# The context block moved to second place in the first layer, and a later start for the next modulation

## The chip, the cores and the metric

The program runs on one core of one Trainium2 chip. The core has five engines that work side by side, each through its own queue in order: PE (TensorE, the matrix unit), DVE (VectorE), ACT (ScalarE), POOL (GpSimd) and SP, which here only starts transfers. Transfers (DMA) are started from the queues of SP and ACT. The metric is the time of one execution on the device in microseconds (us); smaller is better. Three runs of the kernel before were timed, and one execution was profiled.

## The reference

Two layers work on 2048 latent tokens and 256 context tokens of 1024 values. Each layer makes shift, scale and gate out of a condition vector (the modulation: `silu(c) @ w_mod + b_mod`), normalises the tokens, projects them with one matrix, runs four mixers, gates their outputs and projects them back:

```
h = rmsnorm(x) * (1 + scale) + shift            # latent by c, context by c_ctx
parts = split(h @ w_in)                          # q, k, v, z_a, u_f, z_f, b, c, h, z_c, u_p, z_p
o_att = silu(z_a) * attention(q, k, v)           # latent reads context + latent, context reads context
o_f   = silu(z_f) * (real(fft2(u_f)) @ w_fourier)
o_c   = silu(z_c) * (b * conv3(c * h))
o_p   = silu(z_p) * pooled(u_p)
x = x + gate * (concat(o_f, o_att, o_c, o_p) @ w_out)
```

The second layer needs of the context only its keys and values, and only the latent tokens are returned. So the context's output (attention, local mixers, projection) is computed in the first layer alone.

## The kernel before

The tokens lie in five blocks: block 0 is the context (256 tokens), blocks 1 to 4 are 512 latent tokens each. Products of f32 accuracy are made of three f16 matmuls (`PASSES`). A layer runs in these stages, and generators hand each stage's work out in small steps, so that two stages can be woven together:

- **Token groups**: `prep` normalises and transposes a block, `token_groups` makes queries, keys, values and the Fourier input and writes them to DRAM (`qd`, `kd`, `vd`, `ud`).
- **Gates with Fourier** (`gate_groups`, `fourier`): the gates are 148 steps of six 128x512 matmuls on PE (L319). The Fourier mixer is 24 steps: for each of two halves nine output rows (`emit`, L753), then six mixing steps. Each `emit` step splits its operands on ACT and DVE (`split_r`, L687 and L688) and runs a few small matmuls (`dft`, L711). `spread` (L1216) puts 136 of the gate steps between the 24 Fourier steps, and `issue_after` ties the order of the two kinds of matmuls on PE: the gate matmuls of one step stay behind the Fourier matmuls of a step some four places earlier.
- **Modulation of later use** (`modulate`, L163): in the first layer, eight columns of modulation run in the same stage, handed out by `weave` (L1227). Each of 32 steps loads 512 KB of `w_mod` (SP queue, L175) and multiplies it by the condition on two streams: the first on DVE (L182, L184); the second on ACT (L187, into one buffer `part`), added up on POOL (L189). Only PE's instructions are tied by `issue_after`; those of DVE, ACT, POOL and SP are put where the scheduler of the framework finds them ready, the earlier traced first.
- **Attention with local mixers and the first part of the projection** (`attention`, `local_groups`, `project`): for each block and each of four heads, `Head.front` finds the largest score of each query row (matmul L958, reduction on DVE L959; 20 such products for a latent block, 2 for the context), and `Head.main` goes over the keys (18 tiles of 128, the context 2), with two exponentials on ACT and the difference of the two on POOL or DVE. The front of the next head is spread over the main loop of the present one, six units ahead. `spread` puts fill steps between: gates left over, local mixers, then the projection of the blocks in `early`.
- **Rest of the projection with the next layer's token groups**: the last two of `blocks` (`late`) are projected while the next layer's tokens are prepared.

The order of the blocks in attention and projection is the list `blocks`, in which the context stood last:

```
blocks = sorted(layer_blocks(L), key=lambda b: b == 0)     # 1, 2, 3, 4, 0
early = blocks[:-2]                                        # 1, 2, 3
late = project(L, blocks[-2:], ...)                        # 4, 0
```

The number of fill steps in attention is `m - 20`, with m growing by a sixteenth of the tokens of `early`. `set_gate` (L1118) makes the gate row of one stream by two f32 matmuls (L1125) and two ACT copies (L1126), and `project` calls it when the stream of the tokens changes. `local_groups` goes by `layer_blocks(L)`, that is 0 to 4.

Of the kernel before, what the change touches and what calls it, by code (L numbers as in the profile page):

```python
# [42 lines left out]
def hybrid_kernel(ctx: ExitStack, tc: tile.TileContext, T, out):  # L43
# [24 lines left out]
    def ring(*tags):  # L68
        i = [0]

        def bank(dt=F32):
            i[0] += 1
            tag = tags[i[0] % len(tags)]
            return banks[tag].tile([128, 2048 // mybir.dt.size(dt)], dt, tag=tag, name=tag)

        return bank

    st_bank, mx_bank, pv_bank, fl_bank = (ring(t) for t in ("st", "mx", "pv", "fl"))
# [149 lines left out]
    def alloc_h(b):  # L228
        n = BLK[b][1]
        per = 2048 // n  # L230
        hT[b] = [[big([128, per, n], F16, f"h{b}{part}{i}") for i in range(KC // per)] for part in range(2)]

    def h_ap(b, part, k, t0, n, nk=1):
        per = 2048 // BLK[b][1]
        t = hT[b][part][k // per]
        return t[:, k % per, t0:t0 + n] if nk == 1 else t[:, k % per:k % per + nk, t0:t0 + n]

    def rms_scale(ss, n, count, tag):
        ms = sm.tile([128, 8], F32, tag=tag, name=tag)[:, 0:n]
        POOL.tensor_scalar(out=ms, in0=ss, scalar1=1.0 / count, scalar2=EPS, op0=ALU.mult, op1=ALU.add)  # L240
        POOL.tensor_tensor(out=ms, in0=ms, in1=nh[:, 0:n], op=ALU.pow)
        return ms

    def prep(L, b, tp, psum):

        s = 1 if b == 0 else 0
        g0, n = BLK[b]

        def load(t):
            xt = tp.tile([128, D], F32, tag="x", name="xt")  # L250
            (SP if L == 0 and b < 2 else ACT).dma_start(out=xt, in_=source(L, g0 + t * 128))
            return xt

        ahead = load(0)
        for t in range(n // 128):
            xt = ahead
            if (t + 1) * 128 < n:
                ahead = load(t + 1)
            xn = tp.tile([128, D], F32, tag="xn", name="xn")
            ss = sm.tile([128, 1], F32, tag="ss", name="ss")  # L260
            ACT.activation(out=xn, in_=xt, func=ACTF.Square, accum_out=ss)
            rstd = rms_scale(ss, 1, D, "rx")
            ACT.activation(out=xn, in_=xt, func=ACTF.Copy, scale=rstd)
            yield
            if t == 0:
                alloc_h(b)
            for half in range(2):
                pt = psum()
                for j in range(4):
                    k = 4 * half + j  # L270
                    PE.transpose(out=pt[:, j * 128:(j + 1) * 128], in_=xn[:, k * 128:(k + 1) * 128], identity=id32)
                h32 = tp.tile([128, 4, 128], F32, tag="h32", name="h32")
                for j in range(4):
                    k = 4 * half + j
                    DVE.tensor_scalar(out=h32[:, j, :], in0=pt[:, j * 128:(j + 1) * 128], scalar1=aff[L][0][:, 0, k, s:s + 1],
                                      scalar2=aff[L][0][:, 1, k, s:s + 1], op0=ALU.mult, op1=ALU.add)
                hi = h_ap(b, 0, 4 * half, t * 128, 128, 4)
                ACT.copy(out=hi, in_=h32)
                POOL.tensor_tensor(out=h_ap(b, 1, 4 * half, t * 128, 128, 4), in0=h32, in1=hi, op=ALU.subtract)  # L279
# [74 lines left out]
    def layer_blocks(L):  # L354
        return list(range(5)) if L == 0 else list(range(1, 5))
# [773 lines left out]
    def source(L, tok):  # L1129

        if L > 0:
            return xd[tok:tok + 128]
        return T["ctx"][tok:tok + 128] if tok < NCTX else T["x"][tok - NCTX:tok - NCTX + 128]
# [42 lines left out]
    def steps(gen, n):  # L1176
        for _ in range(n):
            if next(gen, 0) == 0:
                return

    def chain(*gens):
        for g in gens:
            yield from g
# [4 lines left out]
    with ExitStack() as st:  # L1188
        tp = TagPool(st, tc, "s0", {**TOKEN, "x": 4, "xn": 2, "h32": 2, "row": 1})
        ws = []  # L1190
        ahead = prep(0, 0, tp, aux_bank)
# [16 lines left out]
        for b in range(5):  # L1208
            ahead = prep(0, b + 1, tp, aux_bank) if b + 1 < 5 else iter(())
# [14 lines left out]
            with tc.issue_after(past[0]), tc.issue_after(load_mark[0] or past[0]):  # L1224
                steps(fill, n * (i + 1) // total - n * i // total)

    def weave(gen, n, other, m):  # L1227

        for i in range(n):
            steps(gen, 1)  # L1230
            steps(other, m * (i + 1) // n - m * i // n)
            yield
        yield from gen
        yield from other

    def opening(load, att):

        for _ in load:
            steps(att, 3)
            yield 1  # L1240

    for L in range(DEPTH):
        blocks = sorted(layer_blocks(L), key=lambda b: b == 0)
        nb = len(blocks)
        GATES = 148 * nb // 5
        zst = ExitStack()
        w_mode(f"g{L}", False)
        gates = gate_groups(L, TagPool(zst, tc, f"z{L}", {"z": 1}), gate_w[L])
        with ExitStack() as st:
            tags = {"acc0": 1, "acc1": 1, "part": 1} if L == 0 else {}  # L1250
            tags.update({"u": 5, "wf": 1, "wm": 2, "t32": 3, "td": 3, "osb": 1, "dtab": 1, "tab": 1, "pq800": 1, "pq801": 1, "pq810": 1, "pq811": 1})
            if L:
                tags.update({"dtab": 2, "tab": 2, "td": 4})
            fp = TagPool(st, tc, f"f{L}", tags)
            mods = chain(*(modulate(i, c, pv_bank, fp) for i, c in ([(0, 4), (0, 5)] + [(1, c) for c in range(6)] if L == 0 else [])))
            work = weave(fourier(L, fp), 24, mods, 32)
            steps(gates, 12)
            spread(work, gates, 24, GATES - 12, 4, True)
            steps(work, 1 << 30)
            if L == 0:  # L1260
                affine(1)
        right = ExitStack()
        ap = TagPool(right, tc, f"a{L}", {"zt": 2, "p32": 2, "qb": 2, "qhh": 3, "qlm": 2, "ph": 3, "pl": 3, "acc": 1, "o32": 1}, "right")
        kvs = {}
        att = attention([Head(L, kvs, b, h, ap) for b in blocks for h in range(4)])
        with ExitStack() as st:
            lp = TagPool(st, tc, f"l{L}", {"e": 8, "ht": 2, "hb": 2, "hu": 2, "pw32": 1, "pw": 2, "dh": 1, "dl": 1})
            early = blocks[:-2]
            out1 = project(L, early, big, 1)
            fill = chain(gates, local_groups(L, lp, out_weights(L), lambda: project_setup(L, kvs, 1), out1), out1)  # L1270
            load = keys_values(L, ap, kvs)
            steps(fill, 5)
            spread(load, fill, 5, 10, 0, True)
            spread(opening(load, att), fill, 6, 18, 1, True)
            n = 28 - 18 + sum(72 if b else 8 for b in blocks)
            m = 2 * 8 * 4 * nb - GATES + 3 - 15 - 18 + sum(BLK[b][1] // 16 for b in early)
            spread(att, fill, n, m - 20, 1)
            project_setup(L, kvs, 2)
            steps(att, 1 << 30)
        zst.close()  # L1280
        right.close()
        with ExitStack() as st:
            pp = TagPool(st, tc, f"p{L}", {"mix": 1, "ml": 2, "gate": 1, "x": 2})
            late = project(L, blocks[-2:], lambda shape, dt, name: pp.tile(shape, dt, "mix" if name == "dg" else name, name), 2)
            steps(late, 1)
            steps(fill, 1 << 30)
            if L + 1 < DEPTH:
                w_mode(f"t{L + 1}", True)
                with ExitStack() as st2:
                    sp = TagPool(st2, tc, f"s{L + 1}", {**TOKEN, "s": 2, "x": 2, "xn": 1, "h32": 2}, "right")  # L1290
                    with tc.issue_after(load_mark[0]):
                        block = token_groups(L + 1, sp, [])
                    for b in blocks[0:2]:
                        for _ in prep(L + 1, b, sp, mx_bank):
                            steps(late, 3)
                    for i, b in enumerate(blocks):
                        ahead = prep(L + 1, blocks[i + 2], sp, mx_bank) if i + 2 < 5 else iter(())
                        if i == 3:
                            gate_w[L + 1] = load_w(L + 1, *GATE_W[0:2], True)
                        for _ in block(b):  # L1300
                            steps(ahead, 1)
                            steps(late, 8)
                        steps(ahead, 9)
                        if i == 0:
                            steps(late, 1 << 30)
            steps(late, 1 << 30)
# [98 lines left out]
```

## Time and profile before

| what | value |
|---|---|
| median of 3 runs | 2219.25 us (2217.25 to 2222.85) |
| the profiled execution's own time | 2221.17 us |
| its span, first to last instruction | 2219.4 us |
| PE busy | 2136.6 us, 96% of the span |
| DVE, ACT, POOL busy | 1411.0, 1216.8, 931.7 us |
| mean granted TensorE clock | 0.990 |

Read it so: PE is busy nearly all the time, and what is not busy is 82.8 us in small pieces. The granted clock is 1.0 (2.4 GHz) but for a few stretches at 0.5 (1.2 GHz), which stand inside the busy time.

### The profile page before, as it was taken

How to read it: one execution, taken by the hardware profiler on the slowest of the kernel's cores; microseconds unless marked ns; L12 is line 12 of the kernel's file. 1: busy time of each engine (PE TensorE's matmuls, PEld its weight loads, DVE VectorE, ACT ScalarE, POOL GpSimd, SP SyncE). 2: the span in 40 equal slices, each digit the busy share in tenths (PEclk: the TensorE clock that was granted, in tenths of full speed). 3: DMA queues.
4: the chain of work that ended last, by engine and by line, in shares of the span. 5: the costliest groups of instructions: out<-in, count | busy, mean ns of one | idle time of the engine just before them, and what ended most of it. 6: DMA issues, size and time to landing. Idle time of an engine off the chain costs nothing. (4 is left out here: it accounts for less than half of the span.)

```text
span 2219.4 us, 41113 instructions
## 1 busy us (share of the span) xinstructions
PE 2136.6 (96%) x16207; PEld 1287.1 (58%) x16207; DVE 1411.0 (64%) x2661; ACT 1216.8 (55%) x2265; POOL 931.7 (42%) x998
## 2 busy tenths in 40 slices
PE   7999989989999999999899999999999999989999
PEld 3998545655556555555456995555455555555544
DVE  3654777456687878676575554522678787877533
ACT  4653445346677767555554534334477676766600
POOL 2786543214455556233233862001356355543300
PEclk9999989999999999999999999999999999999999
DMA  8433554551212122222454333335221221223133
GB/s 324 141 101 96 178 165 160 203 155 48 65 46 69 58 71 79 95 71 69 171 200 134 118 100 114 110 105 169 71 65 33 68 63 46 72 88 99 42 102 123
DMA packets 182639, 237.95 MB, mean 107 GB/s; under 512 B 47178, under 2 KB 132526, under 8 KB 182446
## 3 DMA queue, kind: packets, MB, share of 16 engines
q1 hardware_dynamic: 159854, 205.96, 28.4%
q10 hardware_dynamic: 22592, 29.37, 4.2%
q8 instruction: 127, 2.08, 0.4%
q14 instruction: 66, 0.54, 0.1%
HBM read 161.48 MB, written 69.34 MB: 104 GB/s over the span
## 5 line engine op out<-in xcount | busy, mean ns | idle before, releaser
L319 PE MATMUL fl<-h,w 128*128 128x512 f16 (+1 forms) x2592 | 595.5, 368 | 0.4 <-ACT z L504 0.2
L1007 POOL TENSOR_TENSOR pl<-p,ph 128x512 f16<-128x512 f32 (+1 forms) x292 | 355.2, 1216 | 517.9 <-ACT p L1006 435.0
L319 PEld LDWEIGHTS <-w 128*128 128x128 f16 x3456 | 331.2, 99 | 362.0 <-issue 38.8
L1005 ACT ACTIVATE ph<-st 128x512 f16<-128x512 f32 (+1 forms) x584 | 348.7, 597 | 239.2 <-PE st L1001 213.3
L959 DVE TENSOR_REDUCE mp<-mx 128x1 f32<-128x512 f32 (+1 forms) x648 | 394.7, 627 | 114.4 <-PE mx L958 111.7
L1166 PE MATMUL fl<-wo,ml 128*128 128x512 f16 x1632 | 378.9, 380 | 1.4 <-ACT gate L1126 1.1
L1006 ACT ACTIVATE p<-st 128x512 f32<-128x512 f32 (+1 forms) x584 | 349.0, 598 | 25.2 <-DVE pl L1007 23.7
L1007 DVE TENSOR_TENSOR pl<-p,ph 128x512 f16<-128x512 f32 (+1 forms) x292 | 233.1, 798 | 83.5 <-ACT p L1006 67.9
L1166 PEld LDWEIGHTS <-ml 128*128 128x128 f16 x1632 | 158.9, 98 | 184.2 <-issue 6.4
L995 PEld LDWEIGHTS <-ph 128*128 128x128 f16 x2320 | 169.6, 98 | 124.3 <-ACT ph L1005 26.8
L995 PE MATMUL pv<-V,ph 128*128 128x130 f16 x2320 | 222.7, 220 | 11.3 <-ACT ph L1005 10.9
L958 PE MATMUL mx<-kst,qhh 128*128 128x512 f16 x512 | 188.1, 379 | 15.2 <-DVE mp L959 12.2
L319 PE MATMUL st<-h,w 128*128 128x512 f16 (+1 forms) x864 | 195.4, 376 | 3.6 <-DVE r L436 3.6
L1000 PE MATMUL st<-qhh,kst 128*128 128x512 f16 x512 | 193.9, 379 | 2.5 <-ACT p L1006 2.3
L1001 PE MATMUL st<-qlm,k 65*128 65x512 f16 x512 | 195.1, 381 | 0.0
L993 PE MATMUL pv<-V,pl 128*128 128x66 f16 x2320 | 169.1, 193 | 4.1 <-DVE pl L1007 2.1
L342 PEld LDWEIGHTS <-h 128*128 128x128 f16 x1632 | 159.9, 98 | 20.6 <-POOL h L279 0.7
L993 PEld LDWEIGHTS <-pl 128*128 128x128 f16 x2320 | 132.6, 97 | 44.0 <-POOL pl L1007 6.0
L1171 DVE TENSOR_TENSOR fl<-fl,gate 128x512 f32<-128x512 f32 x68 | 47.4, 697 | 99.8 <-PE fl L1166 99.7
L145 POOL TENSOR_TENSOR root<-root,ph__105 128x2 f32<-128x2 f32 (+1 forms) x28 | 20.3, 726 | 207.6 <-DVE root L144 197.7
L157 ACT ACTIVATE ml<-mix,f 128x1024 f16<-128x1024 f32 x34 | 39.1, 1151 | 113.6 <-PE fl L1166 80.3
L332 PEld LDWEIGHTS <-h 128*128 128x128 f16 x1728 | 98.5, 98 | 0.7
(300 smaller groups left out, 3024.4 us busy)
## 6 DMA issues: line engine op xcount, KB each, us to landing
wm<-in_w_mod_dram SPq DMA_DIRECT2D x48, 512.0 KB, 4.5
wst<-in_w_in_dram SPq DMA_DIRECT2D x44, 512.0 KB, 4.2
mix<-mixd SPq DMA_DIRECT2D x34, 512.0 KB, 4.4
zd<-z SPq DMA_DIRECT2D x64, 256.0 KB, 2.2
wst<-in_w_out_dram SPq DMA_DIRECT2D x32, 512.0 KB, 4.5
xd<-x SPq DMA_DIRECT2D x18, 512.0 KB, 3.0
xt<-xd ACTq DMA_DIRECT2D x18, 512.0 KB, 4.4
x<-in_x_dram SPq DMA_DIRECT2D x16, 512.0 KB, 5.2
```

The costliest lines, as they stand in the source:

```text
L319: last = PE.matmul(out=ps, lhsT=w[:, wp, k, :], rhs=h_ap(b, hp, k, 0, n), start=(k == 0 and i == 0), stop=(k == KC - 1 and i == 2))
L342: PE.matmul(out=ps[:, t], lhsT=h_ap(b, hp, k, (2 * i + t) * 128, 128), rhs=w[:, :, wp, k, :], start=(k == 0 and j == 0), stop=(k == KC - 1 ...
L958: mark[0] = PE.matmul(out=ps, lhsT=qhh[:, t * 128:(t + 1) * 128], rhs=kk, start=True, stop=True).ins
L959: DVE.tensor_reduce(out=mp[:, t, i:i + 1], in_=ps, axis=AX.X, op=ALU.max)
L993: PE.matmul(out=pv[t // 2][:, t % 2, 0:66], lhsT=p, rhs=v[:, 0:66], start=False, stop=(kt == nk - 1), skip_group_check=True)
L995: PE.matmul(out=pv[t // 2][:, t % 2, :], lhsT=p, rhs=v, start=(kt == 0 and t % 2 == 0), stop=False, skip_group_check=True)
L1000: mark[0] = PE.matmul(out=ps, lhsT=self.k_tile(0, kt), rhs=qhh, start=True, stop=False).ins
L1001: PE.matmul(out=ps, lhsT=self.k_tile(1, kt)[0:65, :], rhs=qlm[0:65, :], start=False, stop=True)
L1005: ACT.activation(out=ph, in_=ps, func=ACTF.Exp, scale=1.0 / LOGIT)
L1006: ACT.activation(out=p32, in_=ps, func=ACTF.Exp, scale=1.0 / LOGIT)
L1007: (POOL if kt % 2 == 0 else DVE).tensor_tensor(out=pl, in0=p32, in1=ph, op=ALU.subtract)
L1166: PE.matmul(out=ps, lhsT=ml[:, mp, k, :], rhs=wo[k][:, wp, half * 512:(half + 1) * 512], start=(k == 0 and j == 0), stop=(k == KC - 1 and ...
```

## The change

In the first layer the list of blocks becomes 1, 0, 2, 3, 4, so the context comes second in attention, `early` becomes 1, 0, 2 and `late` 3, 4. The next layer's token groups keep their order 1, 2, 3, 4, 0 through a list of its own. `local_groups` itself is not touched by the diff. `weave` gets a parameter: the modulation's 32 steps are handed out over the Fourier steps 6 to 23 in place of 0 to 23.

```diff
-    def weave(gen, n, other, m):
+    def weave(gen, n, other, m, alone):
 
         for i in range(n):
             steps(gen, 1)
-            steps(other, m * (i + 1) // n - m * i // n)
+            if i >= alone:
+                steps(other, m * (i + 1 - alone) // (n - alone) - m * (i - alone) // (n - alone))
             yield
...
     for L in range(DEPTH):
-        blocks = sorted(layer_blocks(L), key=lambda b: b == 0)
+        blocks = [1, 0, 2, 3, 4] if L == 0 else layer_blocks(L)
+        order = [1, 2, 3, 4, 0]
...
-            work = weave(fourier(L, fp), 24, mods, 32)
+            work = weave(fourier(L, fp), 24, mods, 32, 6)
...
-                    for b in blocks[0:2]:
+                    for b in order[0:2]:
                         for _ in prep(L + 1, b, sp, mx_bank):
                             steps(late, 3)
-                    for i, b in enumerate(blocks):
-                        ahead = prep(L + 1, blocks[i + 2], sp, mx_bank) if i + 2 < 5 else iter(())
+                    for i, b in enumerate(order):
+                        ahead = prep(L + 1, order[i + 2], sp, mx_bank) if i + 2 < 5 else iter(())
```

## Rows read from the trace of the kernel before

**Rows 1.** The page, part 1: busy time, share of the span, instructions.

```profile
PE 2136.6 (96%) x16207; PEld 1287.1 (58%) x16207; DVE 1411.0 (64%) x2661; ACT 1216.8 (55%) x2265; POOL 931.7 (42%) x998
```

**Rows 2.** Stretches: us, busy us (instructions) per engine, clock, DMA share, GB/s.

```profile
240.40:244.05 3.65, 0.00 (x0) 0.00 (x1) 1.20 (x7) 1.32 (x4) 2.82 (x2) 1.00 0.61 180
244.50:251.30 6.80, 6.36 (x24) 4.47 (x24) 4.14 (x14) 3.00 (x6) 0.76 (x2) 0.50 0.48 158
284.70:299.10 14.40, 10.19 (x52) 5.07 (x51) 14.40 (x33) 7.54 (x14) 7.57 (x6) 1.00 0.52 174
299.10:312.80 13.70, 12.48 (x49) 8.99 (x50) 9.35 (x22) 4.86 (x11) 3.67 (x3) 0.50 0.55 177
500.00:1035.00 535.00, 524.59 (x4248) 299.25 (x4247) 404.76 (x653) 351.77 (x676) 253.44 (x258) 1.00 0.21 66
1074.00:1095.00 21.00, 17.15 (x120) 9.54 (x118) 12.82 (x43) 8.14 (x25) 6.60 (x12) 0.99 0.21 71
1094.40:1097.80 3.40, 2.92 (x7) 1.02 (x7) 0.73 (x3) 1.27 (x3) 0.78 (x2) 0.50 0.70 224
1097.80:1200.00 102.20, 101.51 (x559) 56.00 (x558) 64.91 (x136) 53.41 (x75) 34.78 (x44) 1.00 0.55 184
1200.00:1335.00 135.00, 135.00 (x1624) 123.59 (x1623) 68.03 (x164) 54.50 (x92) 91.07 (x106) 1.00 0.34 107
```

**Rows 3.** Timeline around the first Fourier matmul: start, us, engine, line, idle before.

```profile
239.90 2.79 POOL L189 TENSOR_TENSOR acc<-acc,part 128x512 f32<-128x512 f32 x1 [1.98 <-ACT part L187]
240.29 0.48 DVE L728 TENSOR_TENSOR tr<-ftmp 128x128 f32<-128x128 f32 x2
242.73 0.72 ACT L187 ACTIVATE part<-wm,sc 128x512 f32<-128x512 f32 x1 [2.90 <-POOL acc L189]
244.05 0.51 PE L711 MATMUL mx<-tab,trd 128*128 128x256 f32 x2 [3.67 <-ACT trd L687]
```

**Rows 4.** Timeline of ACT around 283 us.

```profile
283.26 0.72 ACT L187 ACTIVATE part<-wm,sc 128x512 f32<-128x512 f32 x1 [2.67 <-POOL acc L189]
...
285.48 0.72 ACT L187 ACTIVATE part<-wm,sc 128x512 f32<-128x512 f32 x1 [0.43 <-POOL acc L189]
```

**Rows 5.** Timeline of POOL, DVE and PE before the matmul at 300.32.

```profile
297.95 1.37 POOL L189 TENSOR_TENSOR acc<-acc,part 128x512 f32<-128x512 f32 x1 [0.83 <-ACT part L187]
298.12 1.34 DVE L688 TENSOR_TENSOR tid<-ti,tid 128x128 fp32r<-128x128 f32 x1
...
300.19 0.28 DVE L688 TENSOR_TENSOR trd<-tr,trd 128x128 fp32r<-128x128 f32 x1
...
300.32 0.58 PE L711 MATMUL mx<-tab,trd 128*128 128x256 f32 x1 [2.99 <-DVE tab L688]
```

**Rows 6.** Waits, 205 to 330 us: us in total, times, longest.

```profile
ACT part L187 <- POOL acc L189: 12.4, 11, 2.9
```

**Rows 7.** The modulation's adds on POOL: ns min/median/max, first and last start.

```profile
L189 POOL TENSOR_TENSOR acc<-acc,part x42: 1261/1320/2793, 220.4 to 378.7; 128x512 f32<-128x512 f32 x42
```

**Rows 8.** Last query store (L462, SP) and Fourier loads (L721, ACT): landings, issues.

```profile
DMA to landing us min/median/max: 2.5/2.9/5.0
...
DMA to landing us min/median/max: 4.1/4.3/6.2
...
218.59 0.39 SPq L462 DMA_DIRECT2D qd<-qo  x1
...
223.69 0.37 ACTq L721 DMA_DIRECT2D u<-ud  x1
```

**Rows 9.** Score reductions, gate matmuls, gate wait, one fill step of six matmuls.

```profile
L959 DVE TENSOR_REDUCE mp<-mx x648: 398/680/693, 469.0 to 2068.7; 128x1 f32<-128x512 f32 x128, 128x1 f32<-128x256 f32 x34
...
L1125 PE MATMUL fl<-dg,ones x20: 590/592/697, 844.3 to 2097.9; 128*128 128x512 f32 x20
...
PE fl L1166 <- ACT gate L1126: 1.1, 1, 1.1
...
1076.05 1.46 PE L1166 MATMUL fl<-wo,ml 128*128 128x512 f16 x6
```

## The prediction

> **What bounds the kernel now.** I read the page first: PE is busy for 96% of the span [rows 1], so a new order of the same work can win only what PE loses. It loses in two ways: it stands idle, or it works at the lower clock. The table of stretches, put together from the granted clock and from PE's gaps, shows where the two parts of this change lie [rows 2]. In the Fourier stage PE stands still from 240.40 to 244.05, and the clock is at 0.5 (1.2 GHz) in the 6.8 us that follow; from 284.7 to 301 there is a second cluster of gaps, 4.2 us of idle and 1.2 more, and again the clock is at 0.5, for 13.7 us. At the end of attention, where the four context heads run, 21.0 us hold 17.15 us of PE work, and 3.4 us at clock 0.5 follow. Elsewhere little is to be had: the body of attention has PE busy for 524.59 of 535 us, the rest of the projection for 101.51 of 102.20 and the next layer's token groups for 135.00 of 135 [rows 2]. Half-clock work counts as busy, but costs about half its stretch.
>
> Then I read the timelines at the two clusters, to see what PE waited for. At the first, the operands of the first Fourier matmul (tr) start on DVE at 240.29, but ACT's queue has the modulation's `part` in front of their cast, and at 242.73 that has waited 2.90 us for POOL's add, which takes 2.79 us. PE starts at 244.05, after 3.67 us [rows 3]. At the second, ACT stands behind the same kind of add for 2.67 us [rows 4], and then DVE: a 128x128 subtraction takes 1.34 us where its twin takes 0.28, and it starts while POOL's add runs (297.95, 1.37 us) and ends with it. PE waits 2.99 us there [rows 5]. So in both clusters it is the modulation's second stream, on ACT and POOL, that stands in front of the Fourier steps.
>
> **The start of the modulation, part by part.** No operation is added or removed: 32 loads of 512 KB, and their work on DVE, ACT and POOL, among it 42 adds, now from 220.4 to 378.7 us [rows 7]. What moves is their place in the order traced.
>
> First cluster: without adds in front, ACT would not have held its queue for those 2.90 us, and the casts would come some 3 us sooner. The Fourier loads would come sooner too: they are issued at 223.69, when the last query store (issued at 218.59) has landed after 5.0 us, the longest of its line (median 2.9), and they land after up to 6.2 us (median 4.3) [rows 8]; the modulation's loads run beside both. These two are worth up to 2.1 + 1.9 = 4.0 us more; I use them only as margin. The idle goes: 3.65 us, and the 0.44 us of PE time missing from the next 6.80 [rows 2], 4.1 together. The low clock follows the gap directly, and half of its 6.8 us is 3.4. Bounds: 0 (the adds run there anyway) and 7.5 us; I take 7.5.
>
> Second cluster: 4.2 + 1.2 = 5.4 us idle and half of 13.7 us = 6.85 at most, at least nothing. These are Fourier steps 6 and 7, where the modulation now begins, so a part stays. I take the one gap of 2.99 us that an add directly lengthens, and half of the clock loss, 3.4: 6.4 us.
>
> What covers the rest: later in the stage the Fourier matmuls may lag some four places, each 5.7 gate steps of about 1.3 us (six matmuls show 1.46 us from first start to last end, overlapped at the edges [rows 9]), so some 29 us of gate matmuls hide a late cast. With that cover gone, each blocked cast costs PE up to 2.9 us as above. The weight loads for later gates, which share four staging buffers and SP's queue with the modulation, now stand ahead of its loads and are earlier, not later.
>
> **The context block, part by part.**
>
> *Taken from the end.* The window 1074 to 1095 has 3.85 us idle. 1.1 us of it is PE waiting for the first late gate row [rows 9], which stays; 2.75 us go, and half of the 3.4 us of low clock, 1.7. Block 4's last head is then followed by projection of block 3, whose inputs are long in DRAM, and by 20 untied fill steps. Together: 4.45 us gained.
>
> *Put in the middle.* The same chains of four short heads run between blocks 1 and 2: again 2.75 us. New is the front of block 2's first head. It now falls into the two main steps of the last context head, where before it was spread over 18. Its 16 reductions of 0.68 us and 4 of 0.40 are 12.5 us on DVE; its matmuls on PE are about 16 x 0.22 + 4 x 0.11 = 3.9 us (a sixth of a fill step for each 512 columns), and the tied fill steps beside it are 2 x 202/306 x 1.3 = 1.7 us. Fill of later steps may not overtake, since it is tied behind those matmuls, and block 2's main loop waits for the last reduction. With nothing run ahead, PE loses 12.5 - 3.9 - 1.7 = 6.9 us and about 1.2 for the transposes after it: 2.75 + 8.1 = 10.8 us. With all run ahead, 2.75 us. There are three buffers for the queries, so this load can start when the second context head is done, and perhaps half the reductions run beside the last two heads: 6.2 us against 2.0 + 1.7 us of PE, 2.5 us idle. I take 5.25 us. A gap of this size has elsewhere been followed by low clock; the smallest such stretch here costs 1.7 us (bounds 0 and 3.4). I take 1.7.
>
> *The gate rows.* `early` now goes latent, context, latent: three gate rows in place of one; `late` needs one in place of two. One more `set_gate`: four recorded matmuls of 0.59 us, 2.4 us at most, 0 if they fall into a gap. I take 2.4; the DVE product and the two ACT copies hide under the 48 matmuls of the tile before.
>
> *The fill moved.* `early` has 10 token tiles, not 12, so 16 fill steps (21 us of PE) go from attention to the rest of the projection, whose two stretches have no idle PE [rows 2]: the sum is the same where both are full. The body of attention idles 10.4 us now; with 202 fill steps for 218 I scale this up by 8%, 0.8 us. With the tiles go their DMAs on SP (mixed rows and x, 512 KB each, and the store of x). Late stores of block 3 now come before the next layer's load of it (ACT's queue), but two of its four tiles are done before that load is first traced, so nothing waits. Nor do other loads there.
>
> **The sum.** -7.5 - 6.4 - 4.45 + 5.25 + 1.7 + 2.4 + 0.8 = -8.2 us against the span of 2219.4. What lies around the span (1.8 us) stays. The median of the runs, 2219.25, stands 1.9 us below the profiled 2221.17; on the median this gives **2211 us**.
>
> **The rivals.**
>
> *The modulation doesn't move.* Only PE is tied, and ACT took modulation work at 242.73 just because its Fourier operand was not ready. If two or three loads still run early and their adds meet the Fourier start, the first 13.9 us are not won and the rest, +5.7, stands: 2225 us, within 0.3% (6.7 us, about what a measurement of this kernel can tell from no change). For: the scheduler ran Fourier loads of the second half far ahead too. Against: with fewer staging buffers before the next weight load, at most two of the modulation's loads find a place early.
>
> *The stall moves.* The two-stream columns, 24 of the 32 steps, had 18 Fourier steps and now have 13.5. One round, `part` and add, takes 2.22 us (283.26 to 285.48 [rows 4]); 42 rounds are 93 us in 158 us before, in about 119 after. So ACT's queue is held more often than its 12.4 us in 125 [rows 6]. If the first cluster goes (-7.5), the second stays and one like the half of it arises (+6.4), then with +5.7 the time is 2224 us: same. The Trainium skill, "SBUF — State Buffer", section "Who interferes with whom", says that a DVE instruction with two SBUF inputs and a GpSimd instruction reading SBUF exclude each other, and the later one blocks for the whole instruction. The trace agrees with that rule in the 1.34 us subtraction [rows 5]. By it, denser adds meet more of the Fourier splits, which speaks against the change.
>
> *Slower: the dense front.* If nothing of block 2's front runs ahead, its place, between the last context head and block 2, costs 10.8 us and 3.4 of low clock. With the end's gain, the gate row and the fill this is +12.95; it decides if the Fourier stage gives back less than 6.3 us. With nothing given back: 2232 us. For it: the reductions of DVE are the only work without a way around; against it: the query buffers allow an early start.
>
> **Chances and range.** Forecast (both clusters shrink, the middle costs some 5 us) 0.43; the modulation doesn't move 0.17; the stall moves 0.16; the dense front 0.24. So faster by over 0.3% 0.43, within it 0.33, slower 0.24. Lower end: both clusters gone (7.5 + 12.2), the middle at 2.75 with no low clock: -18.2 us, 2201. Upper end 2232. As each of these ends is a case by itself, 2200 to 2230 leaves one in ten on each side. The forecast's own range is 2201 to 2213.
>
> **What would show it.** In the profile after: no gap of over 1 us before the first Fourier matmul, and clock 1.0 in the 15 us after it; POOL's adds (L189) first starting after about 260 us, or, if the rival is right, still at 220. The second cluster smaller, or moved by 30 to 60 us. Attention ends without idle PE before the late gate row. Between blocks 1 and 2 a stretch of reductions (L959) back to back, with PE idle 3 to 11 us. 24 recorded gate matmuls in place of 20. It is wrong if PE idles longer in later Fourier steps than it did in the two clusters, or if the context heads idle in the middle by more than 11 us.

## The result and the profile after

The changed kernel takes 2229.72 us (median of 8 runs, 2227.12 to 2237.06), the kernel before 2218.47 beside it (8 runs, 2216.31 to 2224.81): a ratio of 1.0052, 95% interval 1.0038 to 1.0066. It is slower by 0.5%, some 11 us, where 2211 was forecast.

The profiled execution took 2234.08 us, 4.4 above the median. Page, part 1, of the kernel after, for [rows 1]: PE has four matmuls more, and 10.8 us more busy time. Four gate matmuls of 0.59 us make 2.4 of that; the rest goes with the lower mean clock (0.985 for 0.990), at which the same work takes longer.

```profile
PE 2147.4 (96%) x16211; PEld 1287.6 (58%) x16211; DVE 1399.8 (63%) x2662; ACT 1216.8 (55%) x2267; POOL 936.3 (42%) x998
```

The stretches tell where the time went. First the two stages of the kernel before: gates with the Fourier steps, and everything from the first head's main loop to the end of the next layer's token groups.

```profile
205.20:450.20 245.00, 233.84 (x1258) 138.22 (x1256) 166.52 (x335) 112.33 (x222) 95.44 (x77) 0.96 0.54 172
458.00:1335.60 877.60, 853.46 (x7077) 530.22 (x7076) 599.21 (x1082) 515.33 (x952) 406.47 (x447) 1.00 0.29 93
```

The same two of the kernel after, then pieces of them, in the columns of [rows 2].

```profile
206.70:442.70 236.00, 228.46 (x1259) 134.19 (x1257) 162.47 (x335) 109.89 (x218) 95.09 (x77) 0.98 0.53 174
453.10:1345.40 892.30, 865.05 (x7081) 533.52 (x7080) 592.68 (x1080) 515.78 (x955) 409.91 (x446) 0.99 0.29 92
...
244.20:251.00 6.80, 5.86 (x15) 2.56 (x16) 3.80 (x17) 3.96 (x10) 1.26 (x1) 0.50 0.67 212
284.70:299.10 14.40, 13.98 (x90) 8.96 (x90) 14.29 (x24) 6.48 (x17) 5.86 (x4) 1.00 0.66 211
442.70:453.10 10.40, 7.86 (x36) 3.48 (x37) 2.07 (x10) 8.07 (x16) 0.25 (x2) 0.84 1.12 348
592.20:630.60 38.40, 38.40 (x327) 22.10 (x326) 16.96 (x35) 29.29 (x58) 21.49 (x24) 1.00 0.20 60
630.60:650.00 19.40, 13.85 (x86) 6.96 (x84) 15.55 (x34) 9.11 (x23) 8.76 (x13) 0.83 0.29 68
650.00:669.30 19.30, 14.38 (x56) 5.73 (x55) 14.48 (x31) 3.60 (x10) 4.43 (x6) 0.77 0.22 69
1050.00:1091.70 41.70, 41.70 (x331) 23.00 (x329) 18.76 (x35) 27.88 (x50) 14.36 (x14) 1.00 0.33 108
...
633.30:636.70 3.40, 3.40 (x17) 1.72 (x16) 3.29 (x7) 0.36 (x2) 1.46 (x1) 0.50 0.00 0
646.90:650.30 3.40, 3.35 (x12) 1.40 (x12) 1.77 (x6) 0.38 (x1) 1.65 (x2) 0.51 0.43 105
657.20:664.00 6.80, 5.87 (x14) 2.16 (x14) 4.69 (x9) 0.72 (x2) 0.00 (x0) 0.50 0.03 12
667.40:674.20 6.80, 6.16 (x25) 3.08 (x26) 5.59 (x11) 3.75 (x8) 2.95 (x5) 0.50 0.30 92
```

The Fourier stage is 9.0 us shorter, the opening of attention after it 2.6 longer (7.8 before, 10.4), and attention with the rest of the projection 14.7 longer. The start (1.5) and the second layer (3.1) make up the 12.9 us by which the span grew. These are two single traces; how far a stage differs between traces with the same modulation comes under "The modulation".

The 14.7 us have a place. From the first context tile (630.60) to block 2's first main step (669.30) PE stands still for 5.55 + 4.92 = 10.5 us, and the granted clock is 0.83 and 0.77; the head before, 38.40 us, has no idle PE at all, while DVE is busy for only 16.96 us of it. The end of attention, where [rows 2] had 3.85 us of idle, now has none. DVE's timeline in that place shows block 2's reductions (L959, 128x512): none starts before 650.63, 20 us after the first context tile, when PE makes the last context head's last scores (650.43).

```profile
647.82 0.40 DVE L959 TENSOR_REDUCE mp<-mx 128x1 f32<-128x256 f32 x1
...
650.63 1.29 DVE L959 TENSOR_REDUCE mp<-mx 128x1 f32<-128x512 f32 x2 [1.44 <-PE mx L958]
...
656.02 2.21 DVE L959 TENSOR_REDUCE mp<-mx 128x1 f32<-128x512 f32 x4
658.58 2.99 DVE L959 TENSOR_REDUCE mp<-mx 128x1 f32<-128x512 f32 x5 [0.34 <-PE mx L958]
...
664.79 2.48 DVE L959 TENSOR_REDUCE mp<-mx 128x1 f32<-128x512 f32 x4 [1.66 <-PE mx L958]
```

PE's longest waits there, 630 to 674 us, come to 8.2 us: ten short ones for those reductions, 3.4 us together, one of 2.1 us for a query load, two for the low half of the exponentials (`pl`), and one for `qb`, which closes the front. So the reductions are waited for in a third of the idle time only. The place has two halves: up to the last scores of the context heads, the heads' own chain, PE idles 5.6 us, and from there to block 2, the front, 4.9.

```profile
PE mx L958 <- DVE mp L959: 3.4, 10, 0.6
PE mx L958 <- DMA qhh<-qd: 2.1, 1, 2.1
PE pv L993 <- DVE pl L1007: 1.5, 2, 1.3
PE mx L967 <- DVE qb L964: 1.2, 1, 1.2
```

Four stretches in and around it, the last rows of the table above, are at the lower of the two clock levels, 3.4 + 3.4 + 6.8 + 6.8 us; half of that, 10.2 us, is what they cost as long as PE has work in them (it is busy for 18.78 of the 20.4 us).

In the Fourier stage the adds of the modulation start as early as before (222.8 us; 220.4 in [rows 7]), though the modulation is traced six steps later. That holds for the first few alone: six adds start before the first Fourier matmul, where seven did, but from 245 to 285 us there is one in place of ten. The adds, for [rows 7], then POOL's time on them (instructions) from 245 to 285 us, before and after:

```profile
L189 POOL TENSOR_TENSOR acc<-acc,part x42: 1261/1301/1863, 222.8 to 396.5; 128x512 f32<-128x512 f32 x42
```

```profile
245.00:285.00 40.00, 13.33 (x10) 0.92 0.48 154
245.00:285.00 40.00, 1.26 (x1) 0.93 0.39 122
```

The timeline around the first Fourier matmul, for [rows 3]:

```profile
241.59 1.55 DVE L728 TENSOR_TENSOR ftmp<-u 128x128 f32<-128x128 f32 x2
241.67 1.32 POOL L189 TENSOR_TENSOR acc<-acc,part 128x512 f32<-128x512 f32 x1 [0.83 <-ACT part L187]
...
244.48 0.48 DVE L728 TENSOR_TENSOR tr<-ftmp 128x128 f32<-128x128 f32 x2
244.79 0.50 ACT L687 CAST trd<-tr 128x128 fp32r<-128x128 f32 x2 [3.19 <-DVE tr L728]
...
245.14 0.80 PE L711 MATMUL mx<-tab,trd 128*128 128x256 f32 x2 [3.98 <-ACT trd L687]
```

The first gap stays (3.98 us for 3.67), and so do the 6.8 us of low clock behind it. What has changed is the releaser: ACT now waits for DVE's `tr`. The two subtractions at 241.59 take 1.55 us, where the two that make `tr` take 0.48, and they end as POOL's add ends. So the trace agrees again with the rule that the prediction cited (the Trainium skill, "SBUF — State Buffer", "Who interferes with whom"). The lengthening is 1.1 us, a part of the 3.98. The second cluster (284.7 to 299.1) is gone.

### The profile page after: what moved, and what is told of

It reads as the page before. It is cut to its first block, busy times and chain, and to the rows that moved or that the text cites. A ratio compares the mean times of both kernels' runs of the same rounds, so it can differ in the third digit from the quotient of the medians.

```text
span 2232.3 us, 41125 instructions
## 1 busy us (share of the span) xinstructions
PE 2147.4 (96%) x16211; PEld 1287.6 (58%) x16211; DVE 1399.8 (63%) x2662; ACT 1216.8 (55%) x2267; POOL 936.3 (42%) x998
## 5 line engine op out<-in xcount | busy, mean ns | idle before, releaser
L1007 POOL TENSOR_TENSOR pl<-p,ph 128x512 f16<-128x512 f32 x292 | 356.3, 1220 | 524.1 <-ACT p L1006 457.1
L1005 ACT ACTIVATE ph<-st 128x512 f16<-128x512 f32 x584 | 348.9, 598 | 250.3 <-PE st L1001 222.8
L959 DVE TENSOR_REDUCE mp<-mx 128x1 f32<-128x512 f32 (+1 forms) x648 | 393.0, 627 | 115.4 <-PE mx L958 112.3
L1006 ACT ACTIVATE p<-st 128x512 f32<-128x512 f32 x584 | 349.5, 598 | 21.2 <-DVE pl L1007 18.7
L1007 DVE TENSOR_TENSOR pl<-p,ph 128x512 f16<-128x512 f32 x292 | 229.3, 785 | 103.8 <-ACT p L1006 82.3
L995 PE MATMUL pv<-V,ph 128*128 128x130 f16 x2320 | 224.1, 221 | 11.5 <-ACT ph L1005 11.2
L958 PE MATMUL mx<-kst,qhh 128*128 128x512 f16 x512 | 189.0, 384 | 14.6 <-DVE mp L959 13.5
L993 PEld LDWEIGHTS <-pl 128*128 128x128 f16 x2320 | 132.9, 97 | 49.7 <-DVE pl L1007 10.5
L145 POOL TENSOR_TENSOR root<-root,ph__105 128x2 f32<-128x2 f32 (+1 forms) x28 | 20.4, 728 | 182.6 <-DVE root L144 173.5
```

What stands on the lines that cost most here:

```text
L958: mark[0] = PE.matmul(out=ps, lhsT=qhh[:, t * 128:(t + 1) * 128], rhs=kk, start=True, stop=True).ins
L959: DVE.tensor_reduce(out=mp[:, t, i:i + 1], in_=ps, axis=AX.X, op=ALU.max)
L993: PE.matmul(out=pv[t // 2][:, t % 2, 0:66], lhsT=p, rhs=v[:, 0:66], start=False, stop=(kt == nk - 1), skip_group_check=True)
L995: PE.matmul(out=pv[t // 2][:, t % 2, :], lhsT=p, rhs=v, start=(kt == 0 and t % 2 == 0), stop=False, skip_group_check=True)
L1005: ACT.activation(out=ph, in_=ps, func=ACTF.Exp, scale=1.0 / LOGIT)
L1006: ACT.activation(out=p32, in_=ps, func=ACTF.Exp, scale=1.0 / LOGIT)
```

## The experiments

Each was timed beside the kernel before on the same chip, in three groups on three chips: `e1_delay`, `e2_order`, `e3_att` and `e6_spread`; `e4_busy`, `e5_lag`, `e7_tied` and `e8_spread_early`; `e9_spread_tied` to `e12_shared`. The medians of the kernel before were 2222.05 (23 runs), 2217.88 (23) and 2221.55 us (24), so ratios are compared, not times. "Attention and projection" is the stretch from the first main step to the end of the next layer's token groups, in one trace each (877.6 us before, 892.3 after); "the place" is that from the first context head's scores to block 2's first main step (38.7 us after, with 10.5 of idle, 5.6 of it in the context heads' own chain).

**The two halves of the change**

`e1_delay`: the later modulation alone.

```diff
-        blocks = [1, 0, 2, 3, 4] if L == 0 else layer_blocks(L)
+        blocks = sorted(layer_blocks(L), key=lambda b: b == 0)
```

> The later modulation alone, with the old order of the blocks. Theory A (the later modulation helps; the front of block 2's first head, pressed into two steps, costs what is lost): the Fourier stage is shorter by about 9 us, as in the changed kernel (3.7 us less idle, 5.1 less low clock), so 2209 to 2213 us, ratio to before about 0.996. Theory B (the longer rest of the projection and the extra gate row cost it): the same here, 2209 to 2213. Theory C (the later modulation itself costs, through its denser adds): 2222 to 2230, ratio 1.002 to 1.005.

Measured: 2220.49 us (11 runs), ratio 0.9993 (0.9981 to 1.0004). The later start alone can't be told from no change, although the Fourier stage is 237.2 us in its trace, 7.8 shorter. The adds start at 223.8 us here too, and the first gap is 4.68 us. In the same trace the opening is 2.7 us longer than before (10.5 for 7.8) and attention and projection 3.9 (881.5 for 877.6).

`e2_order`: the new block order alone.

```diff
-            work = weave(fourier(L, fp), 24, mods, 32, 6)
+            work = weave(fourier(L, fp), 24, mods, 32, 0)
```

> The new order of the blocks alone, with the modulation as it was. Theories A and B: the whole loss without the gain of the Fourier stage, 2229.7 + 9 = 2236 to 2240 us, ratio about 1.009. Theory C: no slower than before, 2217 to 2222.

Measured: 2236.61 us (6 runs), ratio 1.0063 (1.0048 to 1.0077). The order alone costs all that the change costs. In its trace attention and projection take 893.5 us, and the place 37.9, with 10.6 of idle. Over all timed runs, (1 - granted clock) x span is 30.2 us on average, for 21.7 of the kernel before; the mean times are 2236.4 and 2221.7. So of 14.7 us lost, 8.5 go with the clock, and 6.2 with the rest.

`e3_att`: the new order in attention alone; the projection keeps the old one, and the modulation begins at step 0.

```diff
+            plan = sorted(blocks, key=lambda b: b == 0)
-            early = blocks[:-2]
+            early = plan[:-2]
...
-            late = project(L, blocks[-2:], ...
+            late = project(L, plan[-2:], ...
```

> The context second in attention alone: early and late projection keep blocks 1, 2, 3 and 4, 0, and the modulation is as it was. Theory A: nearly as slow as with the whole new order, 2232 to 2240 us, with 30 us or more between the first context tile and the first tile of block 2, about 10 us of it idle, and several stretches at clock 0.5. Theory B: 2216 to 2222, as before, since the projection is as before.

Measured: 2244.74 us (4 runs), ratio 1.0105 (1.0088 to 1.0122). The place is as dense (36.7 us, 11.2 of idle). Part of the loss on top has a place of its own: the late projection now begins with block 4, whose last head has only just ended, and PE waits 1.81 and 0.75 us for x and 1.23 us in between, 3.8 us of some 8. The rest is not explained. So with the new order in attention the projection is better off with the new order too.

```profile
1152.10 5.34 PE L1166 MATMUL fl<-wo,ml 128*128 128x512 f16 x24 [1.81 <-DVE x L1172]
1158.68 0.38 PE L130 MATMUL mx<-sq,ones 128*128 128x2 f32 x2 [1.23 <-ACT w L295]
```

**The dense front**

`e6_spread`: the changed kernel, in which the fronts of the context heads and of block 2's first head are spread evenly over the steps of head (1,3) and the context heads, with four query buffers of their own for the context heads (their tiles are in the diff of `e10_buffers`). The same work, at other places.

```diff
+        mains = [2 if hd.b == 0 else 18 for hd in heads]
+        wants = size[1:] + [0]
+        group = [i for i, hd in enumerate(heads) if hd.b == 0]
+        if group:
+            group = [group[0] - 1] + group
+            cum = lambda k: sum(wants[i] for i in group) * sum(mains[i] for i in group[:k]) // sum(mains[i] for i in group)
+            even = [cum(k + 1) - cum(k) for k in range(len(group))]
+            for i, w in zip(group, even):
+                wants[i] = w
-            want = size[i + 1] if i + 1 < len(heads) else 0
-            n = 2 if hd.b == 0 else 18
+            want, n = wants[i], mains[i]
...
-"qhh": 3, "qlm": 2,
+"qhh": 3, "qlm": 2, **({} if L else {"qhc": 4, "qlc": 4}),
```

> The changed kernel with the fronts of the context heads and of block 2's first head spread evenly over the 18 steps of block 1's last head and the 8 of the context (26 units in those 18 steps in place of 4), and with query buffers of their own for the context heads. Theory A: idle between the first context tile and block 2's first tile falls from 10.5 us to 3 to 5, the low clock there goes (10 us), and the time is 2211 to 2217, faster than before. Theory B, or if the context heads' own chains cost the idle: 2226 to 2232, as the changed kernel.

Measured: 2216.81 us (11 runs), ratio 0.9978 (0.9969 to 0.9987): faster than the kernel before, and the loss of the order is gone. Attention and projection take 875.3 us. The stretches of its trace: the place takes 19.50 us in place of 38.7, with 4.6 of idle, and the head before it, 44.30 us in place of 38.40, carries 30.54 us of DVE work without idle PE. The idle that is left is nearly all the context heads' own chain (4.3 us up to their last scores; 0.3 from there to block 2).

```profile
592.20:636.50 44.30, 44.30 (x371) 25.55 (x369) 30.54 (x61) 30.36 (x60) 23.03 (x26) 1.00 0.24 66
636.50:656.00 19.50, 14.93 (x108) 8.56 (x107) 17.08 (x35) 10.97 (x29) 10.24 (x12) 0.91 0.10 35
```

Its reductions on DVE begin some 15 us before the first context head's scores (636.5):

```profile
621.29 1.88 DVE L959 TENSOR_REDUCE mp<-mx 128x1 f32<-128x512 f32 x3
...
642.22 0.41 DVE L959 TENSOR_REDUCE mp<-mx 128x1 f32<-128x256 f32 x1
```

Three kernels take this apart. `e10_buffers` has the four query buffers alone, with the front where the change put it:

```diff
-            qhh = tp.tile([128, 512], F16, tag="qhh", name="qhh")[:, 0:n]
+            qhh = tp.tile([128, 256], F16, tag="qhc", name="qhh") if b == 0 else tp.tile([128, 512], F16, tag="qhh", name="qhh")
```

(the same for `qlm`, and the tags as above)

> The changed kernel with four query buffers of their own for the context heads and nothing else, so that block 2's first query load need not wait for a context head; the front stays in the last head's two steps. If the dense place sets the loss, only the 2.1 us gap at the query load goes: the stretch from the context heads to block 2 stays at 35 to 39 us and the ratio to the kernel before at 1.003 to 1.006. If the query buffers set it, the stretch falls to some 20 us and the ratio to 0.997 to 0.999.

Measured: 2232.18 us (6 runs), ratio 1.0049 (1.0032 to 1.0067). The place takes 35.1 us with 9.7 of idle. The wait for the query load is gone, but other waits take most of its place: the idle is 0.8 us less. Over the timed runs the buffers alone can't be told from nothing (1.0049 for 1.0052).

`e11_context` spreads over the context heads' steps alone:

```diff
-            group = [group[0] - 1] + group
```

> The spread kernel with the fronts spread over the context heads' eight steps alone, not over the head before them too. The reductions of block 2's first head, 12.5 us of DVE, and those of the context heads then share some 20 us with the heads' own work. If DVE's throughput in that stretch is what TensorE waits for, the stretch comes between the two: 24 to 32 us, idle 5 to 9 us, ratio 1.000 to 1.004. If it is enough that the front isn't held to the last two steps, it is that of the spread kernel: 19 to 21 us, ratio 0.997 to 0.999.

Measured: 2231.34 us (7 runs), ratio 1.0040 (1.0025 to 1.0055), and the place takes 34.9 us with 10.1 of idle. The expected middle course did not come: it is hardly better than the dense front. So it is not shown that DVE's throughput is what PE waits for: DVE is busy for 26.44 of the 34.9 us. DVE's timeline shows how the place came to be as long. The first 128x512 reduction of block 2 is at 653.77, though its steps are traced earlier; before it stand the late 128x256 ones, 11 and 13 us after that at 638.44. The short heads are a chain on several engines (PE's longest wait there, 2.42 us before 643.91, is for ACT's `p`, and ACT had waited 2.15 us for POOL's `pl`), and block 2's products did not run ahead of its end. Why the schedule held them there was not tried further.

```profile
638.44 0.41 DVE L959 TENSOR_REDUCE mp<-mx 128x1 f32<-128x256 f32 x1
649.35 0.41 DVE L959 TENSOR_REDUCE mp<-mx 128x1 f32<-128x256 f32 x1
651.17 0.40 DVE L959 TENSOR_REDUCE mp<-mx 128x1 f32<-128x256 f32 x1
653.77 0.69 DVE L959 TENSOR_REDUCE mp<-mx 128x1 f32<-128x512 f32 x1 [1.67 <-PE mx L958]
```

`e12_shared` has the even spread of `e6_spread` with the three shared buffers (its diff without the last two lines).

> The spread kernel without query buffers of its own: the three shared ones. If the spread does the work, the stretch is 19 to 23 us and the ratio 0.997 to 0.999. If three buffers can't hold the fronts that run ahead, the fronts wait for the heads before them, TensorE idles at the query loads by 2 us a piece, and the ratio is 1.000 to 1.005.

Measured: 2224.39 us (12 runs), ratio 1.0007 (0.9996 to 1.0018); attention and projection take 881.5 us. The spread gives back the greater part of the loss (1.0052 to 1.0007), and the buffers, worth nothing alone, are worth some 6 us with it. The place did not shrink as expected: it begins 10 us earlier and is 38.7 us long, but with more of PE's work in it, 6.8 us of idle and a clock of 0.96. So its length alone is no measure.

```profile
620.20:658.90 38.70, 31.94 (x193) 16.32 (x191) 27.51 (x63) 15.76 (x36) 13.00 (x22) 0.96 0.24 69
```

`e5_lag`: the fill in attention may lag four places.

```diff
-            spread(att, fill, n, m - 20, 1)
+            spread(att, fill, n, m - 20, 1 if L else 4)
```

> The changed kernel, in which the output matmuls woven into attention may lag four places, not one, so that matmuls of later fill may run ahead of the dense front. If TensorE idles because the fill is held behind the front's matmuls, the idle of that stretch falls from 10.5 to under 5 us and the time to 2214 to 2222. If the block's main loop itself waits for the reductions and nothing else is left to run, the stretch keeps its length and its idle, and the time is within 3 us of 2229.7.

Measured: 2230.89 us (5 runs), ratio 1.0070 (1.0056 to 1.0084); the place takes 34.9 us with 11.3 of idle, and attention and projection 896.2. So the prediction's reason that the tied fill "may not overtake" is not what costs the time: untying it by three more places gives nothing back. `spread` also ties the fill behind the latest query load; that tie stayed, and was not tried.

`e4_busy`: the products of block 2's first front are computed three times each.

```diff
-                    mark[0] = PE.matmul(out=ps, lhsT=qhh[:, t * 128:(t + 1) * 128], rhs=kk, start=True, stop=True).ins
+                    for _ in range(3 if self.L == 0 and b == 2 and h == 0 else 1):
+                        mark[0] = PE.matmul(out=ps, lhsT=qhh[:, t * 128:(t + 1) * 128], rhs=kk, start=True, stop=True).ins
```

> The changed kernel, in which each product of the front of block 2's first head is computed three times in place of once into the same place, so that TensorE has some 8 us more work in the stretch in which it stands idle for 10.5 us. If the low clock there is caused by the idle, the stretch from the first context tile to block 2 keeps its 38 to 40 us, holds 2 to 4 us of idle and no low clock beyond that of the gaps left, and the time is 0 to 8 us under the changed kernel's 2229.7. If the low clock has another cause, the clock in the stretch stays near 0.8 and the time is that of the changed kernel or up to 8 us longer. If the stretch is set by TensorE's fill and not by the reductions, it grows by the 8 us.

Measured: 2235.35 us (6 runs), ratio 1.0080 (1.0062 to 1.0098). The stretches of its trace:

```profile
630.60:650.00 19.40, 13.92 (x87) 7.05 (x84) 15.31 (x34) 9.82 (x25) 8.74 (x13) 0.83 0.29 68
650.00:671.30 21.30, 18.39 (x95) 8.59 (x94) 15.23 (x31) 2.88 (x8) 4.43 (x6) 1.00 0.20 63
```

Where the repeated products stand, from 650 on, the clock is 1.00, for 0.77 in the kernel after; in the first part, which is unaltered, it is 0.83 in both. So in this trace the low clock went where PE's idle was filled, and the timed runs agree: (1 - granted clock) x span is 24.6 us over the six runs, 22.0 for the kernel before beside them, and 28.7 for the changed kernel. That won nothing: the added matmuls, some 8.8 us (40 of 0.22, an estimate), took what the clock gave back. The place keeps 8.4 of its 10.5 us of idle, where 2 to 4 were expected, and is 2.0 us longer; attention and projection take 892.3 us, as in the kernel after.

**The modulation**

`e7_tied`: the later modulation alone, tied in the schedule behind the store of the Fourier step before it (`z_mark`), so that its loads can't be taken early.

```diff
-                SP.dma_start(out=zd[row, :, g0:g0 + n], in_=z)
+                z_mark[0] = SP.dma_start(out=zd[row, :, g0:g0 + n], in_=z).ins
...
-                steps(other, m * (i + 1 - alone) // (n - alone) - m * (i - alone) // (n - alone))
+                with tc.issue_after(z_mark[0]):
+                    steps(other, m * (i + 1 - alone) // (n - alone) - m * (i - alone) // (n - alone))
```

> The kernel with the later modulation alone, in which the modulation is also tied in the schedule behind the store of the Fourier step before it, so that its loads can't be taken early. If its early loads and adds set the gap before the first Fourier matmul, the adds begin after 255 us, the gap of 4.0 to 4.7 us and the low clock after it go, and the time falls by 5 to 7 us against 2220.5. If the gap is set by the loads of the Fourier inputs, it stays within 1 us and so does the time. If the stall only moves, the gap goes, gaps of the same sum come up later in the Fourier stage or at the start of attention, and the time is within 3 us of 2220.5.

Measured: 2215.11 us (12 runs), ratio 0.9992 (0.9981 to 1.0003). Now the adds really start later (271.7 us), and the wait before the first Fourier matmul is gone; 1.84 us, for a table, remain some matmuls on. But a gap of 3.20 us stands at 288.8, with 6.8 us of low clock behind it, and the opening takes 9.7 us (7.8 before). The adds, PE's timeline at both places, and the low stretch of that trace, in this order:

```profile
L189 POOL TENSOR_TENSOR acc<-acc,part x42: 1261/1350/2237, 271.7 to 405.4; 128x512 f32<-128x512 f32 x42
```

```profile
247.93 0.39 PE L711 MATMUL mx<-tab,trd 128*128 128x256 f32 x1 [1.84 <-ACT tab L687]
...
292.05 0.80 PE L711 MATMUL mx<-tab,trd 128*128 128x256 f32 x2 [3.20 <-DVE tab L688]
```

```profile
291.10:297.90 6.80, 5.85 (x25) 4.17 (x26) 5.29 (x12) 1.99 (x5) 1.26 (x1) 0.50 0.93 329
```

The stall moves, and the time is what it was, although in this one trace the Fourier stage is 234.7 us, 10.3 shorter than in the kernel before; attention and projection, 881.1 us, take 3.5 of that back, the opening 1.9.

`e8_spread_early`: `e6_spread` with the modulation from step 0.

```diff
-            work = weave(fourier(L, fp), 24, mods, 32, 6)
+            work = weave(fourier(L, fp), 24, mods, 32, 0)
```

> The kernel with the front spread evenly over the head before and the context heads, with the modulation from the first Fourier step on, as in the kernel before. If the later start is worth nothing, the time is within 2 us of the 2216.8 that the same kernel has with the later start; if it is worth the 8 us by which the Fourier stage was shorter in one trace, it is 2222 to 2226. The stretch from the context heads to block 2 stays at 18 to 21 us in either case.

Measured: 2214.45 us (11 runs), ratio 0.9990 (0.9981 to 0.9998), beside 0.9978 (0.9969 to 0.9987) with the later start. The place is 20.5 us. The pair puts the later start at 0.12%, with intervals that overlap.

Three pairs of kernels differ in the start of the modulation alone, and all lean the same way: 0.07% (`e1_delay` and the kernel before), 0.11% (the changed kernel and `e2_order`) and 0.12% (`e6_spread` and this one), 1.6 to 2.7 us. None is clear of its interval by itself. The traces agree: from the first gate matmul to the first main step, Fourier stage and opening together, the four kernels with the early start take 248.0 to 252.8 us, 250.2 on average, the eight with the later start 246.3 to 249.0, 247.4 on average, and the two tied ones 244.5 and 244.9. The Fourier stage alone misleads: in `e6_spread`, with the same modulation as `e1_delay`, it is 242.8 us (237.2 there), and the opening 6.1 (10.5 there). So the later start is worth some 2 to 3 us, an estimate from these pairs and traces, and not the 9 us that the stage of one trace showed.

`e9_spread_tied`: `e6_spread` with the tie of `e7_tied`.

> The kernel with the spread front and the later modulation, in which the modulation is tied behind the store of the Fourier step before it. If the gain of a modulation that really starts later holds where attention no longer loses time, the gap before the first Fourier matmul falls to about 1.8 us, as it did with the old block order, and the time is 4 to 7 us under that of the spread kernel (a ratio of 0.995 to 0.996 to the kernel before). If the stall only moves to later Fourier steps and to the start of attention, the ratio is 0.997 to 0.999, as in the spread kernels without the tie.

Measured: 2215.38 us (12 runs), ratio 0.9976 (0.9963 to 0.9990). The gap before the first Fourier matmul is down to 0.64 us, and one of 3.21 us stands at 286.1, for DVE's `tab` again. It is no faster than without the tie (0.9978). With `e6_spread` it is the fastest here: 0.7% under the changed kernel (0.9976 to 1.0052), and 0.2% under the kernel before, less than the 0.3% that the prediction took as tellable, though the intervals leave 1 out.

## Why the prediction was wrong

The forecast was -8.2 us, and +11.25 was measured. The halves, as `e1_delay` and `e2_order` had them, -1.6 and +14.6, sum to +13.0, which agrees within the intervals.

**The start of the modulation** (-13.9 forecast, some 2 to 3 us found, no pair clear by itself). The step that failed is "without adds in front": it took the order traced for the order run. The rival "The modulation doesn't move" named it in part: the first adds start at 222.8 us, six of them before the first Fourier matmul, and the first cluster keeps its gap and its low clock. The prediction had allowed for "at most two" early loads; five were issued by 238.4. The later adds did move, and the second cluster went, but part of its worth came back as new waits: 2.46 us at 445.9 for `kc` in the opening, and 1.58 us at 346.5 for a modulation sum, each with 3.4 us of low clock behind it (from 449.0 and 350.0). When the modulation was made to move, in `e7_tied`, the other rival came true as well: the stall moved to 288.8. Both rivals had put the Fourier stage near zero in sum, which is near what came. How the opening and attention give back what the stage gains in a trace was not tried.

**Taken from the end** (-4.45): right. [rows 2] had 3.85 us of idle and 3.4 of low clock there; now 41.70 us up to the end of attention are full, and the wait of 1.1 us for the late gate row [rows 9], which the prediction kept, is gone too. A wait of 0.66 us for x stands in the projection, at 1103.1.

**Put in the middle** (+5.25 and +1.7): the step that failed in the order. The forecast took half the reductions to run ahead; none did: no 128x512 reduction starts before the last context head's last scores. The case "with nothing run ahead", 10.8 us, is near the 10.5 us of idle in the trace, but by luck: its parts were 2.75 us for the heads' chain and 8.1 for the front, and the trace has 5.6 and 4.9. The chain of the four short heads, "again 2.75 us", cost twice that in the middle, 2.1 of it the wait for a query load, and the front cost 3 us less than its sum. "Perhaps half the reductions run beside the last two heads" had only the three buffers for it, and `e10_buffers` shows that buffers alone don't move the front. What the front needs is to be spread over the long head before, as `e6_spread` beside `e11_context` shows. That the place lacks DVE's throughput is not shown, and `e11_context` speaks against it: DVE is busy for 30.0 of 38.7 us in the changed kernel and for 26.44 of 34.9 there. What holds block 2's products back stays open.

**The low clock** of that place was mis-sized most: 1.7 us taken and 3.4 as its upper bound, from the smallest such stretch, 10.2 in the trace and, net of what went at the end, 8.5 over the runs of `e2_order`. That stretch stands at the end of attention in the kernel before, where 3.85 us of idle in 21.0, the longest wait 1.1 us, came with one low stretch; here 10.5 us of idle in 38.7, the longest wait 2.1 us, came with four. The bound was taken from a place with less idle.

**The gate row and the fill moved** (+2.4, +0.8): the gate row is there, as 24 recorded matmuls. Neither size is told apart from the rest: the 6.2 us that `e2_order` lost besides the clock are near 10.5 - 3.85 = 6.65 of idle alone. `e3_att` shows that the new order in the projection was right to have.

The rival "Slower: the dense front" had the place and the sum of the idle right, 2232 us if the Fourier stage gives nothing back, and it came to 2229.72. That it came so near is in part luck: the chain and the front were mis-sized against each other, and its low clock was 3.4 us where the trace has 10.2.

## What to carry to other kernels

When short work is put between two long pieces, ask where the next long piece's preparation ran before: if it was spread over a long piece, it must be spread over the one ahead of the short work, with buffers to hold it, or it is pressed into the short work itself (38.7 us here, 19.5 when spread). A generator that is traced later can still begin as early as before, where its first loads find buffers and engines free; look for its first instructions in the trace, and count how many come early. And price a place of many short waits by more than its idle: here the clock took as much again.

## What was not expected of the hardware

Low-clock stretches came in a place where no wait was longer than 2.1 us, and in and around it they cost as much as the idle itself (10.2 and 10.5 us).

How much of a run is at the low clock differs from execution to execution of one kernel: in the 23 runs of the kernel before beside `e1_delay`, `e2_order`, `e3_att` and `e6_spread` the mean granted clock lies between 0.986 and 0.993, which is 15.5 us of a span of 2220 us. So a stretch of one trace, like the 7.8 us that `e1_delay` is shorter in the Fourier stage, is weaker evidence than the timed runs.
